# Two decoder layers on one core: score matmuls of an attention pair first, masks and decays after them, and a new table of priorities

## The chip, the cores and the metric

One Trainium2 chip, one of its cores. The metric is the device time of one execution in microseconds (us). The kernel before takes 358.33 us in the median of 3 runs (357.59 to 359.37).

## What is computed

Two layers over 256 tokens of width 1024. Each projects the modulated input to all queries, keys, values and gates, runs three kinds of attention head beside each other (DSA: 4 heads with an indexer that keeps the 64 best keys; FoX: 6 heads with a decay added to the scores; NSA: 6 heads with a compressed, a selected and a windowed branch), gates their output, projects it back and normalises.

```python
def hybrid_layer(x, c, ...):
    shift, scale, gate = jnp.split(c @ w_ada + b_ada, 3, axis=-1)
    u = x * (1.0 + scale[:, None, :]) + shift[:, None, :]
    h = split_cols(u @ w_in)
    ...
    o_dsa = dsa_mixer(dq, dk, h["dsa_v"], iq, ik, iw)
    o_fox = fox_mixer(fq, fk, fv, logf)
    o_nsa = nsa_mixer(grp(nq), grp(nq_rot), kc, vc, ks, kvs("nsa_vs"), kw, kvs("nsa_vw"), gates)
    mix = jnp.concatenate([o_dsa, o_fox, o_nsa], axis=-1)
    y = (mix * jax.nn.silu(h["gate"])) @ w_out
    return layer_norm(ALPHA * x + (1.0 + gate[:, None, :]) * y, ln_g, ln_b)
```

## The kernel before

**Weights.** All weights stream from HBM through SyncE's queue as tiles `raw` of up to 128x1024 (L497). ScalarE rounds each to `wh` (L528), VectorE takes the rest `wl = raw - wh` (L543), and every projection is three matmuls, h·H, l·H and h·L (L558, L559, L560). Some tiles are not matmul weights but rows of `w_ada`: VectorE multiplies them by `c` and sums them up (L592, called ada here).

**Stages.** In each layer come first the token-major projections (four chunks of columns), then 16 column-major weight tiles T0 to T15 (each 24 matmuls, shown in two halves of 12), between which the attention runs, and then the output projection: four blocks (two halves of the tokens by two halves of the width), each over four weight pieces that are called q0 to q3. Piece q reads the gated attention output `mH`, `mL` of head pairs 2q and 2q+1; for it VectorE multiplies the gate by the heads' output (L1165, L1173), ScalarE rounds to `mH` (L1176), VectorE takes `mL` (L1178).

**An attention pair.** `attn_pair` does two heads at once, 11 times in each layer: 6 pairs of NSA (three, each in two branches), 3 of FoX, 2 of DSA. Its scores are four matmuls over 64 rows (L756): for each half of the queries (t = 0 with 128 keys, t = 1 with 256) and each head a of the pair, in two PSUM tiles of 384 columns, one for each head. On them come, as matmuls over 96 or 128 rows in bf16, the decay (L761, FoX alone) and the mask (L766 for DSA, L768 for the others, 128 columns of the diagonal). In layer 1 the mask isn't a matmul: `vmask=('', 'dfn')` lets VectorE add it while it looks for the maximum (L697). Then follow exp on ScalarE (L703 or L714), the sum's reciprocal on VectorE (L685), the scaling (L727), the transposes (L737), their copy out of PSUM (L741) and the product with the values (L790). In an NSA pair the compressed branch is added last (L1128), and the output is copied to SBUF (L1010).

**What sets the order.** The whole program is recorded by a planner (`Order`): each step asks for an engine and states a duration, each task has a priority, and the planner always takes the step that can start first, by priority among those that can. The priorities, the limits of PSUM banks by use (`acc`, `s`, `side`), the order of the weight tiles (`tord0`, `tord1`), of the output's pieces (`oq0`, `oq1`) and the place of the ada tiles in the stream (`ada_at`) stand in the table `PR` (L373). What comes out is a fixed order on each engine; an instruction that waits holds up all behind it on its engine.

Of the kernel before, what the change touches and what calls it, by code (L numbers as in the profile page):

```python
# [18 lines left out]
P = 128  # L19
# [156 lines left out]
def bcast(ap, axis, n):  # L176
    return ap.unsqueeze(axis).to_broadcast([*ap.shape[:axis], n, *ap.shape[axis:]])
# [5 lines left out]
def stream_order():  # L183
    o = []

    def chunk(c, l):
        o.extend((c, l, q) for q in range(4))
# [10 lines left out]
    for l in range(DEPTH):  # L198
# [12 lines left out]
        else:  # L211
            for c in PR["cord"]:
                chunk(c, l)
        extra = []
        if l == 0:
            a, b = PR["ada_at"]
            extra += [(a + b * j, [("ada", 1, j, h) for h in range(2)]) for j in range(8)]
        a, b = PR["adag_at"][l]
        extra += [(a + b * j, [("ada", l, 2 * j + i, 2) for i in range(2)]) for j in range(4)]
# [18 lines left out]
class Order:  # L238
# [38 lines left out]
    def _unblock(self):  # L277
        moved = True
        while moved:
            moved = False  # L280
            for t in sorted(self.tasks, key=self._key):
# [6 lines left out]
                elif r[0] == "R":  # L288
# [3 lines left out]
                    if cls in ("s", "pt", "o", "ms", "ad"):  # L292
                        side = sum(self.used.get((tag, c), 0) for c in ("s", "pt", "o", "ms", "ad"))
                        if side + n > PR["side"]:
                            continue
# [19 lines left out]
    def run(self):  # L315
        while True:
            self._unblock()
            best = None
            for e in "PAVG":
                cand = [(t["ready"] + self.LAT[e], t) for t in self.tasks if t["req"][0] == e]  # L320
                if not cand:
                    continue
                first = max(self.free_at[e], min(r for r, _ in cand))
                r, t = min((z for z in cand if z[0] <= first + (PR["tol"] if self._key(z[1])[0] <= -2 else 0.02)),
                           key=lambda z: self._key(z[1]))
# [14 lines left out]
def pr(name, l):  # L340
    old = {"npair": ("nsa", 3), "dpair": ("dsa", 2), "fpair": ("fox", 3)}
    if name in old and name + str(l) not in PR:
        return [pr(old[name][0], l) + 0.01 * i for i in range(old[name][1])]
    return PR.get(f"{name}{l}", PR.get(name))
# [25 lines left out]

SCRATCH = 1024
RW = [11, 8]
PR = dict(irow=2, tout=(1, 1), tch=2, vmask=('', 'dfn'), zn='VA', upart=4, ul='VVVV', nrm='AAAA', cord='DCAB', t1q=0, cuts=(0, 512, 1024), oq=(0, 1, 2, 3), tord=(0, 1, 2, 3, 4, 5, 6, 7, 8, 9, 10, 11, 12, 13, 14, 15), gpp=(0, 1), res=-3.5, warm=10, tol=0.02, ada_at=(8, 0.5), adag_at=((0, 0.5), (8, 1)), ow=(512, 256), aff=3.14, tw=512, nact=((0, 0), (1, 0), (0, 1), (1, 1)), pro='', gp0=(0, 1), gp1=(0, 1), acc=4, s=3, pt=1, o=3, ms=3, side=7, topk=3, idx=2, dec=0.5, cmp=1.2, nsa=1.6, dsa=1.7, fox=1.8, gate=0.72, gate1=4.07, ada=9.04, main=10, ev=0, split=5, nahead=1, acc1=1.5, cmp1=2.15, dec0=0.36, nsa1=0.13, topk1=6.18, nsa0=1.72, dec1=1.66, idx1=0.56, tord1=(0, 4, 2, 7, 6, 1, 8, 9, 5, 3, 10, 12, 11, 13, 15, 14), dsa0=0.12, oq0=(3, 1, 0, 2), cmp0=1.01, fox1=1.95, dsa1=4.17, fox0=1.48, oq1=(1, 2, 3, 0), topk0=3.94, tord0=(0, 1, 3, 2, 4, 5, 6, 9, 7, 8, 10, 11, 12, 15, 14, 13), idx0=4.21, nrm1='AAAA', nrm0='AAAA', t1q0=0, t1q1=0, npair1=(-0.28, -0.61, -0.19), fpair1=(0.89, 8.92, 0.42), dpair0=(1.42, 0.27), dpair1=(4.85, 0.02), npair0=(3.8, 1.84, 4.78), fpair0=(1.21, 1.56, 1.31))  # L373


@with_exitstack
def trunk(ctx: ExitStack, tc: tile.TileContext, xT, x, crow, wst, bcol, lnrow, pe_b, cst, cstb, out,
# [3 lines left out]
    V, A, T, G = nc.vector, nc.scalar, nc.tensor, nc.gpsimd  # L381
# [14 lines left out]
    def nm(s):  # L396
        uid[0] += 1
        return f"{s}_{uid[0]}"

    def bank(cls, n=1):  # L400
        return ("R", "b", n, cls, CAP[cls])
# [7 lines left out]
    def until(*names):  # L409
        return ("U", names)  # L410

    def ps(*shape):
        n = int(np.prod(shape))
        t = pp.tile([P, 512], F32, tag="b", name=nm("b"), bufs=8)
        v = t[:, :n]
        if len(shape) == 2:
            v = v.rearrange("p (a b) -> p a b", b=shape[1])
        elif len(shape) == 3:
            v = v.rearrange("p (a b c) -> p a b c", b=shape[1], c=shape[2])
        return v  # L420
# [50 lines left out]
    ident_b = cb[:, 0:P]  # L471
    diag_b = cb[:, P:2 * P]
    esel_b = cb[0:96, 2 * P:2 * P + 6 * P].rearrange("p (h q) -> p h q", q=P)
# [272 lines left out]
    def attn_pair(l, kind, qT, kT, vs, obox, first, last, mask=None, cum=None, gate=None, prio=1):  # L746
        yield until(("raw", ("cb",)), ("raw", ("masks",)))
        yield bank("s", 2)
        onv = kind in PR["vmask"][l]
        yield ("P", 2 * fmm(128, 256) + (0 if onv else 0.35 if mask is not None else 0.24) + (0.35 if cum is not None else 0))  # L750
        sp = [ps(384) for _ in range(2)]
        for t in range(2):
            nk = P * (t + 1)
            for a in range(2):
                r = slice(64 * a, 64 * a + 64)
                T.matmul(sp[a][:, P * t:P * t + nk], qT[r, t * P:(t + 1) * P], kT[r, :nk], start=True,  # L756
                         stop=onv and cum is None, skip_group_check=True)
            for a in range(2):
                so = sp[a][:, P * t:P * t + nk]
                if cum is not None:  # L760
                    T.matmul(so, esel_b[:, cum[1] + a, :], cum[0][:, :nk], start=False, stop=onv,  # L761
                             skip_group_check=True)
                if onv:
                    continue
                if mask is not None:
                    T.matmul(so, ident_b, mask[:, P * t:P * t + nk], start=False, stop=True, skip_group_check=True)  # L766
                else:
                    T.matmul(so[:, nk - P:], ident_b, diag_b, start=False, stop=True, skip_group_check=True)  # L768
        vm = None if not onv else (causal[:, P:], causal) if mask is None else (mask[:, 0:P], mask[:, P:])
        nmx = small([P, 2, 2], "nmx", 6)  # L770
        st = small([P, 2, 2], "st", 6)
        evs = [(nm("exp"),) for _ in range(2)]
        ps_ = [[], []]
        for a in range(2):
            od.spawn(head_exp(sp[a], a, nmx, st, evs[a], ps_[a], vm), prio)
        yield until(*evs)
        yield ("V", 0.18 + (0.16 if gate is not None else 0))
        r = stats_finish(st, gate)
        evs = [(nm("head"),) for _ in range(2)]
        outs = [[], []]  # L780
        for a in range(2):
            od.spawn(head_pt(l, ps_[a][0], r, a, evs[a], outs[a]), prio)
        yield until(*evs)
        yield ("P", 0.85)
        if first:
            obox.append(ps(S))
        O = obox[0]
        for kt in range(2):
            for a in range(2):
                T.matmul(O[64 * a:64 * a + 64, P * kt:], vs(a, kt), outs[a][0][:, 256 * kt:256 + 128 * kt],  # L790
                         start=(first and kt == 0), stop=(last and kt == 1), skip_group_check=True)
        od.release("pT", 2)
# [6 lines left out]
    cum = small([96, S], "cum", 1, dt=BF16)  # L799
# [723 lines left out]
```

## Time and profile before

| | |
|---|---|
| median of 3 runs | 358.33 us |
| profiled execution | 361.92 us, span 360.1 us |
| TensorE busy | 338.1 us (94%), 2308 matmuls |
| VectorE busy | 306.7 us (85%), 757 instructions |
| ScalarE busy | 247.5 us (69%), 640 instructions |
| DMA | 76.51 MB, mean 212 GB/s |
| mean granted TensorE clock | 0.975 |

The profile is one execution. PE is TensorE, DVE VectorE, ACT ScalarE, SP SyncE. Matmuls overlap, so a matmul's listed duration is longer than the time to the next one's start; what one costs is read from the differences between starts. A group "x4" is several records that ran on from one another: a matmul in f32 over 64 rows leaves two records, one in bf16 leaves one. "Idle before" an instruction, with what ended it, is a wait; DVE, ACT and SP work through their rows in order, and so does PE.

### The profile page before, as it was taken

The page shows a single profiled execution, that of the slowest core. Times are in us where ns is not written, and L with a number is a line of the kernel's source. Part 1 is how long each engine was busy: PE and PEld are TensorE (multiplying, and loading weights), DVE is VectorE, ACT ScalarE, POOL GpSimd, SP SyncE. Part 2 cuts the span into 40 slices and gives each one's busy share as a digit, 9 for nine tenths or more (in the row PEclk, how much of TensorE's full clock was granted, in tenths as well). Part 3 has the DMA queues.
Part 4 walks back from the last instruction along what each step waited for, and adds up shares of the span by engine and source line. Part 5 has one row for each costly group of instructions (what it writes and reads, how often), then busy time and mean ns, then how long its engine had stood idle before and what let it go on. Part 6 is the DMA issues. An engine that isn't in the chain of part 4 may idle for free.

```text
span 360.1 us, 6567 instructions
## 1 busy us (share of the span) xinstructions
PE 338.1 (94%) x2308; PEld 275.4 (76%) x2308; DVE 306.7 (85%) x757; ACT 247.5 (69%) x640; POOL 2.5 (1%) x10
## 2 busy tenths in 40 slices
PE   5889999999999999997999999999999999999991
PEld 2668787888878776785888887868888997887890
DVE  4798997999997999999699898889899988467485
ACT  3446464996938888997086884657998857998120
POOL 2000000000000000000000000000000000000000
PEclk9899999999989999996999999999999999999997
DMA  7999999998736475550569386546587572403011
GB/s 218 408 407 406 407 380 392 410 412 331 233 96 212 164 237 174 177 167 0 155 183 308 114 300 206 177 124 192 161 283 238 181 230 60 116 2 117 3 58 58
DMA packets 22537, 76.51 MB, mean 212 GB/s; under 512 B 3028, under 2 KB 3432, under 8 KB 22376
## 3 DMA queue, kind: packets, MB, share of 16 engines
q1 hardware_dynamic: 22216, 75.80, 61.3%
q8 instruction: 18, 0.29, 0.3%
q10 hardware_dynamic: 288, 0.29, 0.2%
q14 instruction: 15, 0.12, 0.1%
HBM read 75.02 MB, written 1.06 MB: 211 GB/s over the span
## 4 chain that ended last, share of the span: by engine, by line
PE 36%; ACT 10%; DVE 5%; issue 1%; DVEq 0%; ACTq 0%
PE b L558 10%; PE b L560 10%; PE b L559 9%; ACT p L703 3%; ACT p L727 3%; DVE wl L543 2%; ACT wh L528 2%; PE b L790 1%; PE b L737 1%; PE b L941 1%; PE b L1045 1%; ACT pT L741 1%; PE b L670 1%; PE b L1418 1%; PE b L756 0%
## 5 line engine op out<-in xcount | busy, mean ns | idle before, releaser
L528 ACT CAST wh<-raw 128x1024 fp32r<-128x1024 f32 (+2 forms) x81 | 82.9, 1038 | 45.4 <-DMA raw<-in_wst_dram 22.1
L543 DVE TENSOR_TENSOR wl<-raw,wh 128x1024 fp32r<-128x1024 f32 (+2 forms) x81 | 96.4, 1195 | 14.2 <-ACT wh L528 12.4
L558 PE MATMUL b<-uH,wh 128*128 128x256 f32 x256 | 77.5, 303 | 0.8 <-ACT g L831 0.8
L560 PE MATMUL b<-uH,wl 128*128 128x256 f32 x256 | 72.6, 284 | 0.4 <-DVE wl L543 0.4
L559 PE MATMUL b<-uL,wh 128*128 128x256 f32 x256 | 72.4, 283 | 0.0
L592 DVE SCALAR_TENSOR_TENSOR raw<-raw,cbc 128x1024 f32<-128x1024 f32 x48 | 58.3, 1218 | 2.9 <-DMA raw<-in_wst_dram 2.5
L558 PE MATMUL b<-wh,uH 128*128 128x512 f32 (+1 forms) x128 | 51.1, 399 | 2.6 <-ACT uH L1398 2.6
L560 PE MATMUL b<-wh,uL 128*128 128x512 f32 (+1 forms) x128 | 50.4, 393 | 2.5 <-DVE uL L1400 2.4
L558 PEld LDWEIGHTS b<-uH,wh 128*128 128x128 f32 x256 | 48.9, 191 | 3.9 <-issue 1.5
L559 PE MATMUL b<-wl,uH 128*128 128x512 f32 (+1 forms) x128 | 49.9, 390 | 0.0
L560 PEld LDWEIGHTS b<-uH,wl 128*128 128x128 f32 x256 | 48.8, 191 | 0.7 <-DVE wl L543 0.7
L559 PEld LDWEIGHTS b<-uL,wh 128*128 128x128 f32 x256 | 49.0, 191 | 0.0
L727 ACT ACTIVATE p<-p,rinv 128x128 f32<-128x128 f32 (+1 forms) x88 | 34.1, 461 | 2.8 <-DVE rinv L685 1.4
L560 PEld LDWEIGHTS b<-wh,uL 128*128 128x128 f32 x128 | 24.4, 191 | 8.9 <-DVE uL L1400 4.6
L558 PE MATMUL b<-wh,mH 128*128 128x512 f32 (+1 forms) x80 | 29.3, 366 | 1.5 <-ACT mH L1176 1.5
L558 PEld LDWEIGHTS b<-wh,uH 128*128 128x128 f32 x128 | 24.4, 191 | 7.8 <-ACT uH L1398 3.2
L560 PE MATMUL b<-wh,mL 128*128 128x512 f32 (+1 forms) x80 | 29.2, 365 | 0.9 <-DVE mL L1178 0.9
L559 PE MATMUL b<-wl,mH 128*128 128x512 f32 (+1 forms) x80 | 28.7, 359 | 0.0
L559 PEld LDWEIGHTS b<-wl,uH 128*128 128x128 f32 x128 | 24.4, 190 | 4.3 <-DVE wl L543 0.3
L741 ACT COPY pT<-b 128x384 f32<-128x384 f32 x44 | 21.4, 489 | 4.7 <-PE b L737 4.5
L790 PE MATMUL b<-pT,vall 128*64 128x256 f32 (+1 forms) x176 | 22.5, 339 | 0.7 <-ACT pT L741 0.7
L737 PE MATMUL b<-cf,p 128*128 128x128 f32 x132 | 22.9, 283 | 0.2 <-ACT p L727 0.2
(179 smaller groups left out, 541.6 us busy)
## 6 DMA issues: line engine op xcount, KB each, us to landing
raw<-in_wst_dram SPq DMA_DIRECT2D x120, 512.0 KB, 5.1
raw<-in_wst_dram SPq DMA_DIRECT2D x7, 480.0 KB, 9.9
lnr<-in_lnrow_dram SPq DMA_DIRECT2D x4, 512.0 KB, 7.3
raw<-in_wst_dram SPq DMA_DIRECT2D x4, 448.0 KB, 3.6
x_sb<-in_x_dram SPq DMA_DIRECT2D x1, 1024.0 KB
row<-gate SPq DMA_DIRECT2D x2, 512.0 KB, 6.0
xT_sb<-in_xT_dram SPq DMA_DIRECT2D x3, 256.0 KB, 10.5
out_dram<-x_sb SPq DMA_DIRECT2D x3, 256.0 KB, 2.2
```

The costliest lines, as they stand in the source:

```text
L528: A.copy(h[:, :n], loaded[key])
L543: (G if on_pool else V).tensor_tensor(lo[:, :n], raw, h[:, :n].bitcast(F32), op=ALU.subtract)
L558: T.matmul(o, ah, bh, start=start, stop=False)
L559: T.matmul(o, ah, bl, start=False, stop=False)
L560: T.matmul(o, al, bh, start=False, stop=stop)
L592: V.scalar_tensor_tensor(w, w, 1.0, cbc, op0=ALU.mult, op1=ALU.mult, accum_out=mods[l][:, j, h:h + 1])
L670: T.transpose(pt[:, i, :], lhs, ident)
L703: A.activation(p_sb[:, blk], p_sb[:, blk], AF.Exp, bias=nmx[:, t, a:a + 1], scale=-1.0, accum_out=st[:, t, a:a + 1])
L727: A.mul(blk, blk, r[:, t, a:a + 1])
L737: T.transpose(pt[:, i, :], p_sb[:, P * i:P * i + P], ident)
L741: A.copy(pT, pt.rearrange("p a b -> p (a b)"))
L790: T.matmul(O[64 * a:64 * a + 64, P * kt:], vs(a, kt), outs[a][0][:, 256 * kt:256 + 128 * kt], start=(first and kt == 0), stop=(last and kt ...
```

## The change

`attn_pair` issues the same four score matmuls first (t = 0 and t = 1 for both heads), and only then, head by head, the decays and the mask. A mask is now one matmul for each head instead of two: for DSA all 384 columns at once, for the others one matmul that repeats the 128 columns of the diagonal and writes them to columns 0 to 127 and 256 to 383 of the head's PSUM tile. Only the first score matmul of a tile has `start` set.

```diff
+        spans = [slice(0, P), slice(P, 3 * P)]
         for t in range(2):
-            nk = P * (t + 1)
             for a in range(2):
                 r = slice(64 * a, 64 * a + 64)
-                T.matmul(sp[a][:, P * t:P * t + nk], qT[r, t * P:(t + 1) * P], kT[r, :nk], start=True,
+                T.matmul(sp[a][:, spans[t]], qT[r, t * P:(t + 1) * P], kT[r, :P * (t + 1)], start=t == 0,
                          stop=onv and cum is None, skip_group_check=True)
-            for a in range(2):
-                so = sp[a][:, P * t:P * t + nk]
+        for a in range(2):
+            for t in range(2):
+                so = sp[a][:, spans[t]]
                 if cum is not None:
-                    T.matmul(so, esel_b[:, cum[1] + a, :], cum[0][:, :nk], start=False, stop=onv,
+                    T.matmul(so, esel_b[:, cum[1] + a, :], cum[0][:, :P * (t + 1)], start=False, stop=onv,
                              skip_group_check=True)
-                if onv:
-                    continue
-                if mask is not None:
-                    T.matmul(so, ident_b, mask[:, P * t:P * t + nk], start=False, stop=True, skip_group_check=True)
-                else:
-                    T.matmul(so[:, nk - P:], ident_b, diag_b, start=False, stop=True, skip_group_check=True)
+            if onv:
+                continue
+            if mask is not None:
+                T.matmul(sp[a], ident_b, mask, start=False, stop=True, skip_group_check=True)
+                continue
+            T.matmul(sp[a].rearrange("p (b n) -> p b n", n=P)[:, ::2, :], ident_b, bcast(diag_b, 1, 2), start=False,
+                     stop=True, skip_group_check=True)
```

The table `PR` gets other numbers for 26 of its entries, among them `acc` 4 to 5, `s` 3 to 2, `side` 7 to 8, `ada_at` (8, 0.5) to (11, 0.25), `ada` 9.04 to 7.25, `oq0` (3, 1, 0, 2) to (3, 0, 1, 2), the two tile orders and the priorities of most pairs. The durations that the planner assumes for a pair are left as they were. VectorE and ScalarE keep all their instructions and shapes; TensorE loses 22 matmuls with their weight loads, all of them masks of layer 0; SyncE keeps its 145 stream entries. Below, what the two recorded orders say in three places; the numbers behind names are buffers.

TensorE, one branch of an NSA pair in layer 0, before (L756 scores, L768 mask with its weight load):

```order
L756 MATMUL b_1522<-q_32_143,q_36_147 128x128
L756 MATMUL b_1523<-q_32_143,q_36_147 128x128
L768 LDWEIGHTS cb
L768 MATMUL b_1522<-cb 128x128
L768 LDWEIGHTS cb
L768 MATMUL b_1523<-cb 128x128
L756 MATMUL b_1522<-q_32_143,q_36_147 128x256
L756 MATMUL b_1523<-q_32_143,q_36_147 128x256
L768 LDWEIGHTS cb
L768 MATMUL b_1522<-cb 128x128
L768 LDWEIGHTS cb
L768 MATMUL b_1523<-cb 128x128
```

The same branch now (the mask is line 769 of the changed file):

```order
L756 MATMUL b_1521<-q_32_143,q_36_147 128x128
L756 MATMUL b_1522<-q_32_143,q_36_147 128x128
L756 MATMUL b_1521<-q_32_143,q_36_147 128x256
L756 MATMUL b_1522<-q_32_143,q_36_147 128x256
L769 LDWEIGHTS cb
L769 MATMUL b_1521<-cb 128x2x128
L769 LDWEIGHTS cb
L769 MATMUL b_1522<-cb 128x2x128
```

The engine goes once, not three times, from matmuls over 64 rows to those over 128 rows or back, and issues two masks, not four.

VectorE, end of layer 0, before: from the third `mL` (of piece q3) to the fourth and last (of q2). `sg` is a gate, `osb` a pair's output, L543 the split of a weight tile.

```order
L1178 TENSOR_TENSOR mL_1760<-sg_2074,mH_1759 128x512
L1173 SCALAR_TENSOR_TENSOR sg_2107<-sg_2107,osb_2116 128x256
L543 TENSOR_TENSOR wl_2134<-raw_1989,wh_2113 128x1024
L1173 SCALAR_TENSOR_TENSOR sg_2107<-sg_2107,osb_1227 128x256
L543 TENSOR_TENSOR wl_2145<-raw_2004,wh_2122 128x1024
L1178 TENSOR_TENSOR mL_1760<-sg_2107,mH_1759 128x512
```

The same stretch now (two lines further down in the file):

```order
L1180 TENSOR_TENSOR mL_1769<-sg_2014,mH_1768 128x512
L543 TENSOR_TENSOR wl_2085<-raw_1912,wh_2058 128x1024
L1167 SCALAR_TENSOR_TENSOR sg_2079<-sg_2079,b_1729 128x512
L543 TENSOR_TENSOR wl_2098<-raw_1931,wh_2087 128x1024
L543 TENSOR_TENSOR wl_2110<-raw_1994,wh_2096 128x1024
L1175 SCALAR_TENSOR_TENSOR sg_2079<-sg_2079,osb_2112 128x256
L543 TENSOR_TENSOR wl_2123<-raw_1997,wh_2102 128x1024
L1175 SCALAR_TENSOR_TENSOR sg_2079<-sg_2079,osb_1234 128x256
L543 TENSOR_TENSOR wl_2128<-raw_2012,wh_2114 128x1024
L1180 TENSOR_TENSOR mL_1769<-sg_2079,mH_1768 128x512
```

The `mL` of q3 has moved up, past three splits and a gate. The last `mL` stands where it stood: as many instructions are ahead of it in both orders; among them were 39 splits and 38 ada rows, now 40 and 37.

TensorE, end of layer 0, before: the last pair's values, its compressed branch, then the output projection, whose first six matmuls are piece q3.

```order
L790 MATMUL b_1887<-pT_2050,vall_135 64x256
L790 MATMUL b_1887<-pT_2077,vall_135 64x256
L790 MATMUL b_1887<-pT_2050,vall_135 64x128
L790 MATMUL b_1887<-pT_2077,vall_135 64x128
L1128 MATMUL b_1887<-pcT_152,vc_151 64x256 x2
L558 MATMUL b_2096<-wh_2030,mH_1759 128x512
L559 MATMUL b_2096<-wl_2059,mH_1759 128x512
L560 MATMUL b_2096<-wh_2030,mL_1760 128x512
```

The same place now:

```order
L792 MATMUL b_1897<-pT_2070,vall_135 64x256
L792 MATMUL b_1897<-pT_2076,vall_135 64x256
L792 MATMUL b_1897<-pT_2070,vall_135 64x128
L792 MATMUL b_1897<-pT_2076,vall_135 64x128
L558 MATMUL b_2052<-wh_2001,mH_1768 128x512
L559 MATMUL b_2052<-wl_2053,mH_1768 128x512
L560 MATMUL b_2052<-wh_2001,mL_1769 128x512
L558 MATMUL b_2052<-wh_2001,mH_1768 128x512
L559 MATMUL b_2052<-wl_2053,mH_1768 128x512
L560 MATMUL b_2052<-wh_2001,mL_1769 128x512
L1130 MATMUL b_1897<-pcT_152,vc_151 64x256 x2
```

Piece q3 now stands ahead of the compressed branch of the last pair, and pieces q0, q1, q2 follow in this order (before: q3, q1, q0, q2).

## Rows read from the trace of the kernel before

**Rows 1.** Stretches: us, then PE, PEld, DVE, ACT, POOL busy (count), PEclk, DMA share, GB/s.
```profile
140.00:160.00 20.00, 20.00 (x157) 16.33 (x156) 19.97 (x42) 18.89 (x55) 0.00 (x0) 1.00 0.57 181
172.00:184.00 12.00, 12.00 (x55) 9.90 (x54) 8.99 (x23) 3.08 (x5) 0.00 (x0) 1.00 0.56 163
301.00:330.00 29.00, 28.77 (x230) 23.82 (x228) 18.81 (x65) 28.83 (x85) 0.00 (x0) 1.00 0.24 67
```

**Rows 2.** Timeline of PE (start us, duration us), layer 0: an NSA branch, first and next.
```profile
91.37 0.49 PE L756 MATMUL b<-q,q 64*128 64x128 f32 x4
...
92.77 0.50 PE L737 MATMUL b<-cf,p 128*128 128x128 f32 x3
```

**Rows 3.** Timeline of PE, layer 0: a FoX pair.
```profile
82.51 0.49 PE L756 MATMUL b<-f,f 64*128 64x128 f32 x4
...
83.91 0.28 PE L761 MATMUL b<-cum,cb 96*128 96x256 bf16 x1
84.03 0.22 PE L768 MATMUL b<-cb 128*128 128x128 bf16 x1
84.09 0.27 PE L761 MATMUL b<-cum,cb 96*128 96x256 bf16 x1
...
84.26 0.49 PE L670 MATMUL b<-cf,chunk 128*128 128x128 f32 x3
```

**Rows 4.** Timeline of PE: a DSA pair of layer 0, FoX and DSA of layer 1.
```profile
137.15 0.49 PE L756 MATMUL b<-q,q 64*128 64x128 f32 x4
...
138.58 0.36 PE L558 MATMUL b<-uH,wh 128*128 128x256 f32 x1
...
298.05 0.49 PE L756 MATMUL b<-f,f 64*128 64x128 f32 x4
...
299.47 0.37 PE L558 MATMUL b<-uH,wh 128*128 128x256 f32 x1
...
312.84 0.93 PE L756 MATMUL b<-q,q 64*128 64x128 f32 x8
313.70 0.87 PE L790 MATMUL b<-pT,vall 128*64 128x256 f32 x8
```

**Rows 5.** Timeline of PE, layer 0's output projection, with waits.
```profile
161.80 0.65 PE L1128 MATMUL b<-pcT,vc 15*64 15x256 f32 x4
163.99 0.50 PE L558 MATMUL b<-wh,mH 128*128 128x512 f32 x1 [1.54 <-ACT mH L1176]
...
165.61 0.80 PE L560 MATMUL b<-wh,mL 128*128 128x512 f32 x1 [0.89 <-DVE mL L1178]
...
171.33 0.47 PE L558 MATMUL b<-wh,mH 128*128 128x512 f32 x1
...
184.14 0.39 PE L560 MATMUL b<-wh,mL 128*128 128x512 f32 x1
```

**Rows 6.** Timeline of DVE, the same place.
```profile
164.87 0.69 DVE L1178 TENSOR_TENSOR mL<-sg,mH 128x512 fp32r<-128x512 f32 x1
165.47 0.42 DVE L1173 SCALAR_TENSOR_TENSOR sg<-sg,osb 128x256 f32<-128x256 f32 x1
165.81 1.22 DVE L543 TENSOR_TENSOR wl<-raw,wh 128x1024 fp32r<-128x1024 f32 x1
166.94 0.42 DVE L1173 SCALAR_TENSOR_TENSOR sg<-sg,osb 128x256 f32<-128x256 f32 x1
...
168.41 0.69 DVE L1178 TENSOR_TENSOR mL<-sg,mH 128x512 fp32r<-128x512 f32 x1
```

**Rows 7.** Stretches of 2 us, columns as in the first group.
```profile
100.00:102.00 2.00, 2.00 (x13) 0.93 (x12) 1.81 (x9) 0.56 (x2) 0.00 (x0) 0.50 0.03 8
166.00:168.00 2.00, 2.00 (x6) 1.52 (x6) 2.00 (x3) 1.37 (x2) 0.00 (x0) 0.50 0.00 0
```

**Rows 8.** Waits of DVE, 90 to 140 us: total, times, longest.
```profile
DVE sg L1165 <- ACT sg L1163: 1.3, 1, 1.3
DVE rinv L685 <- ACT p L714: 1.1, 1, 1.1
```

More of the change, by code (lines that the diff above doesn't have):

```diff
@@ L372 @@
 RW = [11, 8]
-PR = dict(irow=2, tout=(1, 1), tch=2, vmask=('', 'dfn'), zn='VA', upart=4, ul='VVVV', nrm='AAAA', cord='DCAB', t1q=0, cuts=(0, 512, 1024), oq=(0, 1, 2, 3), tord=(0, 1, 2, 3, 4, 5, 6, 7, 8, 9, 10, 11, 12, 13, 14, 15), gpp=(0, 1), res=-3.5, warm=10, tol=0.02, ada_at=(8, 0.5), adag_at=((0, 0.5), (8, 1)), ow=(512, 256), aff=3.14, tw=512, nact=((0, 0), (1, 0), (0, 1), (1, 1)), pro='', gp0=(0, 1), gp1=(0, 1), acc=4, s=3, pt=1, o=3, ms=3, side=7, topk=3, idx=2, dec=0.5, cmp=1.2, nsa=1.6, dsa=1.7, fox=1.8, gate=0.72, gate1=4.07, ada=9.04, main=10, ev=0, split=5, nahead=1, acc1=1.5, cmp1=2.15, dec0=0.36, nsa1=0.13, topk1=6.18, nsa0=1.72, dec1=1.66, idx1=0.56, tord1=(0, 4, 2, 7, 6, 1, 8, 9, 5, 3, 10, 12, 11, 13, 15, 14), dsa0=0.12, oq0=(3, 1, 0, 2), cmp0=1.01, fox1=1.95, dsa1=4.17, fox0=1.48, oq1=(1, 2, 3, 0), topk0=3.94, tord0=(0, 1, 3, 2, 4, 5, 6, 9, 7, 8, 10, 11, 12, 15, 14, 13), idx0=4.21, nrm1='AAAA', nrm0='AAAA', t1q0=0, t1q1=0, npair1=(-0.28, -0.61, -0.19), fpair1=(0.89, 8.92, 0.42), dpair0=(1.42, 0.27), dpair1=(4.85, 0.02), npair0=(3.8, 1.84, 4.78), fpair0=(1.21, 1.56, 1.31))
+PR = dict(irow=2, tout=(1, 1), tch=2, vmask=('', 'dfn'), zn='VA', upart=4, ul='VVVV', nrm='AAAA', cord='DCAB', t1q=0, cuts=(0, 512, 1024), oq=(0, 1, 2, 3), tord=(0, 1, 2, 3, 4, 5, 6, 7, 8, 9, 10, 11, 12, 13, 14, 15), gpp=(0, 1), res=-3.5, warm=10, tol=0.02, ada_at=(11, 0.25), adag_at=((0, 0.5), (8, 1)), ow=(512, 256), aff=2.1, tw=512, nact=((0, 0), (1, 0), (0, 1), (1, 1)), pro='', gp0=(0, 1), gp1=(0, 1), acc=5, s=2, pt=1, o=3, ms=3, side=8, topk=3, idx=2, dec=0.5, cmp=1.2, nsa=1.6, dsa=1.7, fox=1.8, gate=0.69, gate1=3.42, ada=7.25, main=10, ev=0, split=5, nahead=1, acc1=1.5, cmp1=0.65, dec0=-0.17, nsa1=0.13, topk1=7.44, nsa0=1.72, dec1=0.47, idx1=0.42, tord1=(0, 7, 4, 6, 2, 1, 8, 9, 5, 3, 10, 12, 11, 13, 14, 15), dsa0=0.12, oq0=(3, 0, 1, 2), cmp0=1.13, fox1=1.95, dsa1=4.17, fox0=1.48, oq1=(2, 1, 3, 0), topk0=3.11, tord0=(0, 1, 3, 2, 4, 6, 5, 9, 7, 8, 11, 10, 12, 14, 15, 13), idx0=4.01, nrm1='AAAA', nrm0='AAAA', t1q0=0, t1q1=0, npair1=(-0.4, -0.19, 2.86), fpair1=(-0.22, 5.77, 3.69), dpair0=(1.78, 2.73), dpair1=(1.61, 2.59), npair0=(3.02, 1.75, 4.78), fpair0=(1.72, 0.16, 1.0))
 @with_exitstack
```

## Prediction

> **What bounds the kernel now.** I read the stretches first, to see which engine is full where, then the timeline of TensorE inside an attention pair for prices, and then the two timelines at the end of layer 0, where the full engines wait for each other. From 140 to 160 us TensorE, VectorE and ScalarE are all nearly full, VectorE with 19.97 of 20 us [rows 1]. What ends this stage is VectorE: TensorE is through with the attention of layer 0 at about 162.4 (161.80 + 0.65) and then stands for 1.54 us for `mH` and 0.89 us for `mL` [rows 5], while VectorE runs on without a gap to the last `mL` at 169.10 (168.41 + 0.69) [rows 6]. After that idleness TensorE's clock is at half (0.50, so 1.2 GHz) [rows 7]: from the third output matmul at 165.61 to the sixteenth at 171.33, 13 steps take 5.72 us; later, 56 steps to the last at 184.14 take 12.81 us, 0.229 us each [rows 5]. From 172 to 184 TensorE alone is full and VectorE has room (8.99 of 12) [rows 1]. Layer 1 is TensorE's nearly throughout, until ScalarE fills up as well from 301 to 330 (28.83 of 29) [rows 1].
>
> **The pairs.** Each price is the time from a pair's first score to the next instruction.
>
> - An NSA branch takes 1.40 us (91.37 to 92.77) [rows 2]. Without masks the eight score records take 0.86 us (312.84 to 313.70) [rows 4], and that stretch also holds the one change back to 128 rows. A bf16 matmul of 256 columns takes 0.12 us (83.91 to 84.03), one of 128 columns 0.06 (84.03 to 84.09) [rows 3]. So a branch will take 0.86 + 2 x 0.12 = 1.10, which saves 0.30; six of them 1.80.
> - A FoX pair of layer 0 takes 1.75 us (82.51 to 84.26) [rows 3] and will take 0.86 + 2 x (0.06 + 0.12 + 0.12) = 1.46: three save 0.87.
> - A DSA pair of layer 0 takes 1.43 us [rows 4] and will take 0.86 + 2 x 0.18 = 1.22: two save 0.42.
> - A FoX pair of layer 1 takes 1.42 us (298.05 to 299.47) [rows 4] and will take 0.86 + 2 x 0.18 = 1.22: three save 0.60. The other eight of layer 1 have no bf16 matmul and keep their price.
>
> That is 3.1 us off TensorE in layer 0 and 0.6 us in layer 1. The mask that is written in two blocks is in no row; its bounds are 0.12 us (the price of as many columns in one block, which is taken, since each block is as wide as today's) and, for the dear end, twice that.
>
> **What of it reaches the end of layer 0.** Not the 3.1 us themselves: VectorE sets the last `mL`, and it keeps every instruction. The same number stands ahead of that `mL` as before, one split more and one ada row less, which I cost at nothing. VectorE gains only what it waits less. In 90 to 140 us two waits of 1.3 and 1.1 us are listed [rows 8]; the second lies behind the stretch at half clock around 101 us [rows 7], where TensorE was late, the first behind a gate's tanh, which the new order puts elsewhere. I take half of the 2.4, so 1.2 us; the bounds are 0 (the new order only moves them) and 2.4 (both go). The last `mL` then ends at 167.9.
>
> The larger term is what TensorE does before that. In the new VectorE order five splits, one gate and two products lie between the third `mL` and the last; by the steps of 0.34 (165.47 to 165.81) and 1.13 (165.81 to 166.94), and 0.60 for `mL` and for the gate, which is as long [rows 6], the two start 0.60 + 5 x 1.13 + 0.60 + 2 x 0.34 = 7.5 us apart, where today it is 3.5. So the third `mL`, which lets piece q3 begin, starts 4.0 us earlier relative to the last, and by 167.9 TensorE can have done q3, q0, q1 and two matmuls of q2: 20 instead of about 10 (by 169.10 today). From the 21st to the 72nd are 51 steps x 0.229 = 11.7 us, which gives 179.6 at full clock.
>
> But TensorE, with 3.1 us less to do, still waits ahead of q3 or ahead of q2, as today, and so I expect the low clock again. Today it costs 5.72 - 13 x 0.229 = 2.7 us; the stretch of half clock from 100 to 102 is shorter, and its 2 us cost 1.0. I take 2.2, near the first, since part of the low clock now falls ahead of the last `mL`, and keep 0 to 2.7. So the 72nd output matmul starts at 179.6 + 2.2 = 181.8 instead of 184.14: 2.3 us earlier. From there TensorE leads and layer 1 follows by as much.
>
> **Layer 1.** 0.6 us less on TensorE; but ScalarE is full from 301 to 330 [rows 1] and has the same rows to do, so I take half, 0.3 us, with 0 and 0.6 as bounds. The last DSA pair now has one half of a weight tile (12 matmuls) less between its scores and its last product; where ScalarE is late, that cover is gone, for at most 12 x 0.12 = 1.4 us, by the step of a 256-column matmul [rows 3].
>
> **What costs nothing.** Sixteen ada loads of layer 1 go one to three weight tiles later into SyncE's queue and so let T8, T10 and T11 pass. The DMA share is 0.57 from 140 to 160 [rows 1] and 0 in the wait at 166 [rows 7], so loads have room there; were a weight tile late, its split and TensorE behind it would be. The other limits of banks act only through the order.
>
> **Sum.** 2.3 + 0.3 = 2.6 us off the profiled execution (361.92 us, 3.59 above the median); taken off the median of 358.33 that is 355.7 us.
>
> **Rivals.**
>
> - *The clock stays high.* If TensorE reaches q3 only just before its `mL`, and its gaps are short, the 2.2 us don't arise: 355.7 - 2.2 = 353.5 us. For it: the work ahead of q2 is now 18 matmuls, not 3. Against: the gap ahead of q2 is still 167.9 less the end of q1; with q3 from about 160.3 on, 18 steps and 0.65 us for L1128 end at 165.1, and it is near 2.8 us, as long as today's two gaps together. The Trainium skill, page "TensorE: Matmul & The Clock Gate", section "What's actually happening", says that the throttled state is the default and activity releases it. By that rule a wait in a new place brings the low clock back, which is the forecast; the half clock after today's gaps agrees [rows 7].
> - *The mask's two blocks cost what the merging saves.* If a mask that writes two blocks takes 0.24 us, the 18 of them (six NSA branches and three FoX pairs, two each) take 2.2 us back and layer 0 saves 0.9 on TensorE; VectorE's waits then stay, and 355.7 + 1.2 = 356.9 us. Against: each block alone is today's mask. The Trainium skill, page "PSUM — Partial Sum Buffer", section "Specifications (TRN2)", says that a non-contiguous access pattern slows matmuls significantly; taken to the letter it speaks against this edit. No row here has such an output, so nothing bears it out yet.
> - *q3 blocks the last pair, and the kernel gets slower.* L1128 of the last pair now stands behind q3 on TensorE. If the third `mL` ends as late as today (165.56), then four more matmuls (0.92), L1128 (0.65), the copy (0.4), and on VectorE product, split, product, split and `mL` (0.34 + 1.13 + 0.34 + 1.13 + 0.69) make the last `mL` end at 171.2, or 172.7 with the first two terms at half clock; 11.7 and 2.2 us later it is 186.6, which is 2.5 us late, less 0.3 for layer 1: 360.5 us. It decides from a third `mL` that ends after about 163.4. For it: the chain is new, and its only slack is the 4.0 us that VectorE's new order gives. Against: that order is fixed, and VectorE has had no gap there.
> - *The order doesn't change what it says* is excluded: the recorded order shows 22 masks fewer and the scores together.
>
> **Chances.** About 0.5%, 1.8 us, is what a measurement of this kernel can tell from no change: faster is below 356.5, slower above 360.1. Forecast 0.42 (355.7, spread about 1.5 by the bounds of VectorE's waits and of the clock: 0.29 faster, 0.13 same); clock stays high 0.18 (0.17, 0.01); mask blocks 0.18 (0.05, 0.13); q3 blocks 0.22 (0.08 same, 0.14 slower). Together 0.51 faster, 0.35 same, 0.14 slower. The range goes from 352.6 (the high clock with most of VectorE's 1.2 us more) to 360.4 (about where q3's blocking lies), with some 0.18 outside; the forecast's own range is 354.2 to 357.2.
>
> **What would show it.** Right: an NSA branch of layer 0 at about 1.1 us and a FoX pair at 1.46; VectorE full from 140 to the last `mL`, which ends near 168; about 20 output matmuls ahead of it; a stretch at 0.50 clock around it. Wrong: a mask's step of 0.2 us or more; TensorE waiting for anything but `mH` and `mL` at the end of layer 0; the last `mL` after 170; new waits of TensorE on L741 after 301 us.

## The result, and the profile after

The changed kernel takes 356.76 us (median of 11 runs, 356.39 to 357.42); the kernel before took 358.59 us beside it (11 runs, 356.99 to 361.62). The ratio is 0.9948, with a 95% interval of 0.9923 to 0.9974. The profiled execution of the changed kernel took 356.42 us with a span of 354.6 us, where that of before took 361.92 us with 360.1. So the two traces differ by 5.5 us and the medians by 1.8. That gap is the key to the rest: the profile shown of before was one of its slower executions.

The stretches of the changed kernel that answer to [rows 1] and [rows 7] (us, then busy time and count of PE, PEld, DVE, ACT, POOL, then the granted clock, DMA share, GB/s):

```profile
140.00:160.00 20.00, 18.12 (x138) 14.31 (x138) 19.96 (x40) 18.41 (x47) 0.00 (x0) 1.00 0.45 162
301.00:330.00 29.00, 28.84 (x210) 23.62 (x209) 16.96 (x46) 26.60 (x73) 0.00 (x0) 1.00 0.22 73
100.00:102.00 2.00, 1.43 (x13) 0.75 (x12) 1.76 (x10) 0.94 (x3) 0.00 (x0) 1.00 0.03 12
166.00:168.00 2.00, 1.98 (x9) 1.64 (x10) 2.00 (x2) 0.18 (x1) 0.00 (x0) 1.00 0.00 0
```

VectorE still fills the end of layer 0 (19.96 of 20 us), and TensorE now has room there (18.12). The two stretches that ran at 0.50, which is 1.2 GHz, now run at 1.00, which is 2.4 GHz.

The pairs, in the timeline of TensorE (start us, duration us): FoX, NSA and DSA of layer 0, then FoX of layer 1, each with the instruction behind it. They answer to [rows 2 to 4].

```profile
81.74 0.93 PE L756 MATMUL b<-f,f 64*128 64x128 f32 x8
82.60 0.34 PE L762 MATMUL b<-cum,cb 96*128 96x128 bf16 x2
82.77 0.27 PE L769 MATMUL b<-cb 128*128 128x256 bf16 x1
82.89 0.33 PE L762 MATMUL b<-cum,cb 96*128 96x128 bf16 x2
...
83.26 0.71 PE L943 MATMUL b<-q,q 32*128 32x128 f32 x8
...
88.77 0.93 PE L756 MATMUL b<-q,q 64*128 64x128 f32 x8
...
89.77 0.36 PE L558 MATMUL b<-uH,wh 128*128 128x256 f32 x1
...
133.75 0.93 PE L756 MATMUL b<-q,q 64*128 64x128 f32 x8
...
134.81 0.42 PE L558 MATMUL b<-uH,wh 128*128 128x256 f32 x1
...
292.19 0.93 PE L756 MATMUL b<-f,f 64*128 64x128 f32 x8
...
293.31 0.36 PE L558 MATMUL b<-uH,wh 128*128 128x256 f32 x1
```

By differences of starts: FoX 1.52 us (1.46 said), NSA 1.00 (1.10 said), DSA 1.06 (1.22 said), FoX of layer 1 1.12 (1.22 said). Part of such a difference belongs to the instruction behind the pair: an NSA branch takes 1.00 us with a weight tile behind it and 1.18 with its product. Compared with the same instruction behind, before and now, the pairs take 1.83 and 1.52 us (FoX), 1.49 and 1.18 (NSA with its product), 1.43 and 1.06 (DSA), 1.42 and 1.12 (FoX of layer 1). So a pair or branch saves some 0.31 us, this DSA pair 0.37. The mask in two blocks takes 0.12 us (82.77 to 82.89), as many columns in one block would.

The end of layer 0 on TensorE answers to [rows 5]:

```profile
157.87 1.25 PE L792 MATMUL b<-pT,vall 128*64 128x256 f32 x8 [1.79 <-ACT pT L741]
159.05 0.50 PE L558 MATMUL b<-wh,mH 128*128 128x512 f32 x1
...
160.64 0.65 PE L1130 MATMUL b<-pcT,vc 15*64 15x256 f32 x4
...
164.94 0.50 PE L558 MATMUL b<-wh,mH 128*128 128x512 f32 x1 [0.72 <-ACT mH L1178]
165.27 0.40 PE L559 MATMUL b<-wl,mH 128*128 128x512 f32 x1
166.02 0.50 PE L560 MATMUL b<-wh,mL 128*128 128x512 f32 x1 [0.35 <-DVE mL L1180]
...
177.71 0.39 PE L560 MATMUL b<-wh,mL 128*128 128x512 f32 x1
```

and on VectorE to [rows 6]:

```profile
157.13 1.29 DVE L1180 TENSOR_TENSOR mL<-sg,mH 128x512 fp32r<-128x512 f32 x2
...
165.28 0.69 DVE L1180 TENSOR_TENSOR mL<-sg,mH 128x512 fp32r<-128x512 f32 x1
```

The last `mL` ends at 165.97 (169.10 before). Exactly 20 output matmuls start ahead of its end: the 21st, at 166.02, is the one that waits for it. The last 512-column output matmul starts at 177.71 (184.14 before).

### The profile page after: what moved, and what is told of

It is laid out like the page before. It is cut to its first block, busy times and chain, and to the rows that moved or that the text cites. A ratio compares the mean times of both kernels' runs of the same rounds, so it can differ in the third digit from the quotient of the medians.

```text
span 354.6 us, 6531 instructions
## 1 busy us (share of the span) xinstructions
PE 331.1 (93%) x2286; PEld 271.1 (76%) x2286; DVE 305.9 (86%) x757; ACT 247.0 (70%) x640; POOL 2.5 (1%) x10
## 3 DMA queue, kind: packets, MB, share of 16 engines
HBM read 75.02 MB, written 1.06 MB: 215 GB/s over the span
## 4 chain that ended last, share of the span: by engine, by line
PE 32%; ACT 10%; DVE 6%; issue 2%; DVEq 0%; ACTq 0%
PE b L558 8%; PE b L559 8%; PE b L560 8%; ACT p L703 3%; DVE wl L543 2%; ACT p L727 2%; ACT wh L528 2%; PE b L792 1%; PE b L737 1%; PE b L943 1%; ACT pT L741 1%; PE b L1047 1%; PE b L670 1%; PE b L756 1%; PE b L1420 1%
## 5 line engine op out<-in xcount | busy, mean ns | idle before, releaser
L543 DVE TENSOR_TENSOR wl<-raw,wh 128x1024 fp32r<-128x1024 f32 (+2 forms) x81 | 96.1, 1193 | 14.0 <-ACT wh L528 11.8
L558 PE MATMUL b<-wh,mH 128*128 128x512 f32 (+1 forms) x80 | 28.5, 356 | 0.7 <-ACT mH L1178 0.7
L560 PE MATMUL b<-wh,mL 128*128 128x512 f32 (+1 forms) x80 | 28.0, 350 | 0.4 <-DVE mL L1180 0.4
L559 PE MATMUL b<-wl,mH 128*128 128x512 f32 (+1 forms) x80 | 27.8, 348 | 0.0
L737 PE MATMUL b<-cf,p 128*128 128x128 f32 x132 | 23.7, 283 | 0.9 <-ACT p L727 0.5
L792 PE MATMUL b<-pT,vall 128*64 128x256 f32 (+1 forms) x176 | 21.6, 339 | 2.1 <-ACT pT L741 2.1
```

Of the source, the lines that this page charges most:

```text
L543: (G if on_pool else V).tensor_tensor(lo[:, :n], raw, h[:, :n].bitcast(F32), op=ALU.subtract)
L558: T.matmul(o, ah, bh, start=start, stop=False)
L559: T.matmul(o, ah, bl, start=False, stop=False)
L560: T.matmul(o, al, bh, start=False, stop=stop)
L737: T.transpose(pt[:, i, :], p_sb[:, P * i:P * i + P], ident)
```

## The experiments

My theory was that the table moves the `mL` at the end of layer 0 and that the edit's own saving is mostly lost to VectorE. The rivals were that the edit is the gain, and that the clock is. The first four kernels ran side by side.

**The kernel before once more.**

> The kernel before, unchanged, for a second profile and the clock of its runs. Theory A (the half clock at the end of layer 0 belongs to the order of the work): the second profile shows a stretch at granted clock 0.50 between 160 and 172 us again, and TensorE's first out-projection matmul again some 1.5 us late; ratio 1.000. Theory B (the profile shown was one of the slow ones, by chance): no stretch at 0.50 there, span near 356 to 357 us, and the runs with the lower mean clock are the longer ones.

358.11 us (12 runs, 356.89 to 361.36). Its profile is another execution of the same program, 357.58 us, without a drop in either place:

```profile
100.00:102.00 2.00, 2.00 (x21) 1.50 (x18) 1.80 (x10) 0.88 (x3) 0.00 (x0) 1.00 0.03 8
166.00:168.00 2.00, 2.00 (x11) 1.65 (x10) 2.00 (x3) 1.86 (x2) 0.00 (x0) 1.00 0.00 0
```

TensorE waits as long for `mH` and `mL` as in [rows 5] (1.5 and 0.9 us), yet the clock stays at 1.00. So the half clock falls in some executions and not in others, and theory B holds for the profile shown. The last `mL` of this second profile, and its 21st and 72nd output matmul:

```profile
166.97 0.68 DVE L1178 TENSOR_TENSOR mL<-sg,mH 128x512 fp32r<-128x512 f32 x1
```

```profile
168.39 0.39 PE L560 MATMUL b<-wh,mL 128*128 128x512 f32 x1
...
179.95 0.39 PE L560 MATMUL b<-wh,mL 128*128 128x512 f32 x1
```

Against the execution of [rows 5, 6], this one has its last `mL` 1.45 us earlier (its end is at 167.65) and its last 512-column output matmul 4.19 us earlier (179.95). The first figure is the delay that the drop near 100 us hands on: of the two waits of VectorE in [rows 8], the one of 1.1 us for `p` is missing here. The other 2.74 us are the drop at the end of layer 0. At full clock the 21st output matmul starts at 168.39 without a wait, 0.74 us after the last `mL`, and 17 have started by its end, not 10.

The unchanged kernel beside it, the same program, had 359.37 us. Where drops come and go, two medians of one program can thus lie 1.3 us apart.

The 99 runs of the unchanged kernel in three comparisons, by their mean clock, show it as well: 16 below 0.9765 have a median of 361.19 us, 56 from there to 0.9855 have 359.38, and the 27 at 0.9855 or above have 357.93. The bands are rough, because the mean also holds the start, where the clock of the first 20 us was between 0.83 and 1.00 in the profiles. All 11 runs of the changed kernel are at 0.986 or above.

**The edit alone**: the new pair code, the old table (against the changed kernel; entries left out are marked by dots).

```diff
-... acc=5, s=2, ... oq0=(3, 0, 1, 2), ...
+... acc=4, s=3, ... oq0=(3, 1, 0, 2), ...
```

> New attn_pair with the old table: the order on the four engines is that of before but for the masks. Theory A (VectorE sets the last mL of layer 0, so TensorE's saving is lost there): pairs of layer 0 at 1.10, 1.46 and 1.22 us, but the first waits for mH and mL grow by about as much as was saved; 0.3 to 1.5 us faster than before (ratio 0.996 to 0.999). Theory B (the edit itself is the gain): as fast as the changed kernel, ratio 0.995 or less, and the table adds nothing.

359.69 us, ratio 1.0010 (0.9989 to 1.0032): it gains nothing that shows, less than theory A's range. The pairs do save what was said, and the waits for `mH` and `mL` at the end of layer 0 have not grown (1.54 and 0.90 us), as theory A had them. What is lost is clock, in two places. One is near 98 us, where a run of thin matmuls (64 rows and 15 columns, then 64 columns, then the 30-column compressed scores) is followed by the scores of a pair. First the undisturbed execution of before, then the edit alone:

```profile
96.40 0.29 PE L1066 MATMUL b<-hid,w_sb 64*64 64x15 f32 x4
96.62 0.55 PE L1070 MATMUL b<-w_sb,hid 64*96 64x64 f32 x4
97.10 0.87 PE L790 MATMUL b<-pT,vall 128*64 128x256 f32 x8
98.19 1.52 PE L1085 MATMUL b<-kc,q 128*128 128x30 f32 x12 [0.22 <-ACT kc L1074]
99.65 0.49 PE L756 MATMUL b<-q,q 64*128 64x128 f32 x4
```

```profile
95.72 0.87 PE L792 MATMUL b<-pT,vall 128*64 128x256 f32 x8
97.43 1.94 PE L1087 MATMUL b<-kc,q 128*128 128x30 f32 x12 [0.84 <-ACT kc L1076]
99.31 1.23 PE L756 MATMUL b<-q,q 64*128 64x128 f32 x6
```

TensorE arrives 1.38 us earlier (95.72 against 97.10), but `kc` comes from ScalarE only 0.76 us earlier, so the wait grows from 0.22 to 0.84 us. Of the 1.38 us, 0.75 are a lead that this execution has at its first pair already (81.79 against 82.54). The other 0.6 us are what the two pairs ahead of this place save, and all of that goes into the wait. The clock is at half from there, and again at the end of layer 0, in this kernel's stretches:

```profile
100.00:102.00 2.00, 2.00 (x12) 1.29 (x11) 1.76 (x10) 0.40 (x2) 0.00 (x0) 0.50 0.03 8
168.00:170.00 2.00, 2.00 (x6) 1.62 (x5) 2.00 (x3) 1.53 (x2) 0.00 (x0) 0.50 0.00 0
```

Of its 12 runs 11 have a mean clock of 0.980 or less; of the 30 of the unchanged kernel beside it, 15 have. The drop at the end of layer 0 is the dearer of the two, as the filled kernels below show.

**The table alone**: the old pair code, the new table (the opposite diff).

> Old attn_pair with the new table: order of VectorE, ScalarE and the queues exactly that of the changed kernel. Theory A: about 20 out-projection matmuls stand ahead of the last mL again, so most of the gain is here: 0.5 to 2 us faster than before (0.994 to 0.999), 0.3 to 1.5 us slower than the changed kernel; pairs at the old prices of 1.40, 1.75 and 1.43 us. Theory B (the edit is the gain): ratio 1.000 to 1.004.

357.48 us, ratio 0.9947 (0.9925 to 0.9969), the ratio of the whole change; 9 of 12 runs at 0.987 or above, and the slowest, 358.87 us, has the lowest clock (0.978). So theory A holds, and the table keeps the low clock away in most runs without the edit. The edit adds to it: this kernel is 0.72 us slower than the changed one, and 0.60 slower than the next kernel, which ran beside it with the scores first. In the traces its last `mL` ends 0.80 us later (166.77 against 165.97), although its first pair starts 0.13 us earlier. What the table does near 98 us shows in the changed kernel, in the same view:

```profile
93.36 0.55 PE L1072 MATMUL b<-w_sb,hid 64*96 64x64 f32 x4
93.84 0.55 PE L737 MATMUL b<-cf,p 128*128 128x128 f32 x3
...
95.64 1.50 PE L1087 MATMUL b<-kc,q 128*128 128x30 f32 x12
```

Three transposes and twelve full matmuls now stand between the two thin groups, and the second waits for nothing.

**Scores first, masks not merged.**

(Arguments left out are marked by dots here and below.)

```diff
-            if mask is not None:
-                T.matmul(sp[a], ident_b, mask, ...)
-                continue
-            T.matmul(sp[a].rearrange("p (b n) -> p b n", n=P)[:, ::2, :], ident_b, bcast(diag_b, 1, 2), ...)
+            for t in range(2):
+                if mask is not None:
+                    T.matmul(sp[a][:, spans[t]], ident_b, mask[:, spans[t]], ...)
+                else:
+                    T.matmul(sp[a][:, 2 * P * t:2 * P * t + P], ident_b, diag_b, ...)
```

> The changed kernel with scores first, but each mask matmul split again into the two of before (22 matmuls more, the same columns, no output in two blocks). Theory A (what the edit saves is the changing between 64-row f32 and 128-row bf16 matmuls, and the columns are the same): an NSA branch stays within 0.1 us of the changed kernel's, and the time within 0.5 us of it. Theory B (a matmul has a fixed price that merging saves, and the two-block output is cheap): 22 times some 0.06 us, about 1.3 us more on TensorE, and 0.5 to 1.3 us slower than the changed kernel. Theory C (the two-block output costs double): faster than the changed kernel by up to 2 us.

356.88 us (7 runs), 0.12 from the changed kernel; a FoX pair takes 1.52 us, as merged, and an NSA branch 1.06:

```profile
88.94 0.93 PE L756 MATMUL b<-q,q 64*128 64x128 f32 x8
89.80 0.40 PE L770 MATMUL b<-cb 128*128 128x128 bf16 x4
90.00 0.36 PE L558 MATMUL b<-uH,wh 128*128 128x256 f32 x1
```

Theory A holds. The same branch with the old pair code, in the kernel with the table alone, has a weight tile behind it too:

```profile
88.66 0.49 PE L756 MATMUL b<-q,q 64*128 64x128 f32 x4
...
90.03 0.36 PE L558 MATMUL b<-uH,wh 128*128 128x256 f32 x1
```

That is 1.37 us. So having the scores together saves 0.31 (1.37 to 1.06), merging the masks some 0.06 more (1.00); where the product follows, merging saves 0.01 (1.19 to 1.18). The branch of [rows 2] can't be set against the 1.00, since its transposes follow it.

**Is it the clock?** Dummy matmuls into a bank that is overwritten next keep TensorE at work where it is thin, and move no other instruction. The two places, for layer 0 only, are ahead of the first compressed scores (three dummies, five with the new pair code) and ahead of the first block's first piece of the output projection (seven):

```diff
+            for _ in range(3 if l == 0 and t == 0 else 0):
+                T.matmul(sw.rearrange("p (b n) -> p b n", n=P), ident_b, bcast(diag_b, 1, 4), start=True, stop=True, ...)
             for j in range(3):
                 T.matmul(sc[:, j], nrT[j][:, t * P:(t + 1) * P], kc_sb, ...)
...
                     mH, mL = mix
+                    for _ in range(7 if l == 0 and n == 0 and t == 0 and q == oq[0] else 0):
+                        T.matmul(acc.rearrange("p (b n) -> p b n", n=P), ident_b, bcast(diag_b, 1, 4), start=True, stop=True, ...)
```

Before, both places filled:

> The kernel before with ten dummy matmuls of 512 columns on TensorE and nothing else moved: three ahead of the twelve 30-column matmuls of the compressed scores near 98 us, seven ahead of the first out-projection matmul of layer 0, where TensorE waits 1.5 us for mH. Theory A (the half clock follows TensorE's thin stretches, and it is what makes before slow): no stretch at 0.50 in either place, mean clock of nearly all runs 0.983 or more, median near that of the runs of before without a drop, 357.9 us (ratio 0.996 to 0.997). Theory B (the drops come from outside this core's work, by chance): clocks of 0.975 to 0.980 in about as many runs as before, ratio 1.000 to 1.002.

357.41 us (356.78 to 357.84), ratio 0.9956 (0.9927 to 0.9985); all 12 runs at 0.988 or above. Ten dummy matmuls make the kernel before 2.0 us faster than the unchanged one beside it (359.39 us), about as much as the whole change. They fit into the waits; `mH` is no longer waited for:

```profile
160.74 1.69 PE L1378 MATMUL b<-cb 128*128 128x512 bf16 x7
162.33 0.50 PE L558 MATMUL b<-wh,mH 128*128 128x512 f32 x1
162.66 0.40 PE L559 MATMUL b<-wl,mH 128*128 128x512 f32 x1
163.95 0.50 PE L560 MATMUL b<-wh,mL 128*128 128x512 f32 x1 [0.89 <-DVE mL L1182]
```

The edit alone, with the place near 98 us filled:

> New attn_pair with the old table and five dummy matmuls of 512 columns ahead of the 30-column matmuls near 98 us, where TensorE waits 0.84 us for kc. Theory A: the drop near 98 us goes, that at the end of layer 0 stays in most runs: mean clocks near 0.984 in place of 0.979, about 1 to 1.5 us faster than the edit alone (358.2 to 358.7 us). Theory B: clocks and time as with the edit alone, 359.4 to 360 us.

359.00 us, slower than theory A's range: 0.7 us gained, not 1 to 1.5. The profile shows the first place at 1.00 and the second at half clock, and only one of the 12 runs lies above 0.984. So the place near 98 us is the smaller part.

The edit alone, both filled:

> As the last, with seven dummy matmuls also ahead of the first out-projection matmul of layer 0. Theory A: no drop in either place, clocks of 0.985 or more, 356.8 to 358.0 us: the edit then gives the 0 to 1 us that the masks save, and the table's gain over the edit alone is mostly the clock. Theory B: time and clocks as with the edit alone. Theory C (the table's order is worth its time at full clock as well): clocks high, and still 1 us or more slower than the changed kernel, 357.8 us or above.

356.93 us (356.45 to 357.81), all runs at 0.987 or above, within 0.2 us of the changed kernel. Theory C falls. In layer 1 the FoX pairs are shorter here than before, too, but a wait for `pT` grows. First the undisturbed execution of before, then this kernel, from 255 to 352 us (total, times, longest):

```profile
PE b L790 <- ACT pT L741: 0.3, 1, 0.3
PE b L792 <- ACT pT L741: 1.0, 2, 0.7
```

The changed kernel, filled near 98 us, as a control:

> The changed kernel with three dummy matmuls of 512 columns ahead of the 30-column matmuls. There is no drop there to take away, so theory A: within 0.5 us of the changed kernel (356.4 to 357.3), the 0.7 us of dummies lost in VectorE's cover at the end of layer 0. Theory B (dummies help or cost by something else than the clock): a change of 0.7 us or more either way.

356.81 us: nothing, as theory A says. So in this kernel dummies bring nothing where there is no drop to prevent.

The edit alone, only the end of layer 0 filled:

> New attn_pair with the old table and seven dummy matmuls ahead of the first out-projection matmul of layer 0 alone, none near 98 us. Theory A (two drops, each with its own price): the drop near 98 us stays, mean clock 0.978 to 0.981; since its delay of TensorE passes on to the end of layer 0, 0.5 to 1.5 us slower than with both places filled (357.4 to 358.4 us), and 1.3 to 2.3 us faster than the edit alone. Theory B (the first drop brings the second about): clocks and time as with the edit alone, 359.4 to 360 us.

357.47 us: the time of theory A, but not its clocks, since only 2 of 12 runs lie at 0.981 or below; the profile has no drop near 98 us although TensorE waits 0.86 us for `kc` there, as with the edit alone. So the first drop comes in a part of the runs. The four kernels with the new pair code and the old table make a square: filling the end of layer 0 gives 2.22 us (359.69 to 357.47) and 2.07 (359.00 to 356.93), filling near 98 us gives 0.69 and 0.54. Only 359.00 and 356.93 ran side by side; the unchanged kernel had 359.37, 359.39 and 359.25 us in the three comparisons. So the two places add as far as can be seen, and the second drop doesn't need the first: with the place near 98 us filled, it still comes.

**Does the order at the end of layer 0 decide?**

```diff
-oq0=(3, 0, 1, 2)
+oq0=(3, 2, 0, 1)
```

> The changed kernel with pieces of layer 0's out projection taken in the order q3, q2, q0, q1: the piece that needs the last mL comes second, so 6 and two matmuls stand ahead of that mL in place of 18 and two. Theory A (how many matmuls stand ahead of the last mL decides, as forecast): 12 x 0.229 = 2.7 us later at the end of the out projection, of which 1 to 2.7 us arrive at the end at full clock; with a wait of some 3.5 us in one piece the half clock comes back in most runs and adds 1 to 2.7: 357.8 to 362 us. Theory B (TensorE isn't the bound after the last mL): 0.5 us at most.

361.21 us, 4.45 more than the changed kernel, and slower than before (1.0046, 1.0020 to 1.0071). Theory A holds, with 8 of 12 runs at 0.980 or below; how the 4.45 us divide between the later start and the low clock this run doesn't show. TensorE stands in one piece ahead of q2, and the clock is at half behind it; timeline and stretch:

```profile
161.12 0.65 PE L1130 MATMUL b<-pcT,vc 15*64 15x256 f32 x4
165.42 0.79 PE L558 MATMUL b<-wh,mH 128*128 128x512 f32 x1 [3.64 <-ACT mH L1178]
```

```profile
166.00:168.00 2.00, 2.00 (x6) 1.21 (x5) 2.00 (x3) 0.66 (x1) 0.00 (x0) 0.50 0.00 0
```

**Layer 1's part of the table set back.** The stretch from the first affine matmul of layer 1 (L631) to the last output matmul is the same to 0.06 us in every trace with one table: 70.11 to 70.17 us with the old one (the kernel before in both profiles and filled, and the edit alone, filled or not), 70.81 to 70.83 with the new one. So the new table costs layer 1 some 0.7 us.

```diff
-gate1=3.42, cmp1=0.65, topk1=7.44, dec1=0.47, idx1=0.42, tord1=(0, 7, 4, 6, 2, ...), oq1=(2, 1, 3, 0), npair1=..., fpair1=..., dpair1=...
+gate1=4.07, cmp1=2.15, topk1=6.18, dec1=1.66, idx1=0.56, tord1=(0, 4, 2, 7, 6, ...), oq1=(1, 2, 3, 0), npair1=..., fpair1=..., dpair1=...
```

> The changed kernel with the table's ten entries for layer 1 alone set back to those of before; those for layer 0 and the common ones stay new. The traces show 70.8 us from the first affine matmul of layer 1 to the last output matmul with the new table and 70.1 with the old one, whichever mask edit. Theory A (the new table costs layer 1 some 0.7 us by the order on ScalarE): layer 0 ends as in the changed kernel, layer 1 takes 70.1 us again, 356.0 to 356.5 us, faster than both kernels. Theory B (the common entries, or work of layer 1 that is hidden in layer 0, set that stretch): 356.7 us or more.

356.13 us (355.50 to 357.08, 12 runs), ratio 0.9928 (0.9899 to 0.9957). The changed kernel's two ends of the stretch, and this kernel's:

```profile
275.54 0.28 PE L631 MATMUL b<-cf,mod 128*8 128x128 f32 x1
...
346.35 0.28 PE L560 MATMUL b<-wh,mL 128*128 128x256 f32 x1
```

```profile
276.57 0.28 PE L631 MATMUL b<-cf,mod 128*8 128x128 f32 x1
...
346.68 0.28 PE L560 MATMUL b<-wh,mL 128*128 128x256 f32 x1
```

70.11 us against 70.81, so the entries for layer 1 cause the 0.7 us; that ScalarE's order does, as theory A has it, wasn't shown, and which instruction gives them wasn't isolated. This kernel has the lowest median of all, by 0.63 us, which fits the 0.7; but it didn't run side by side with the changed kernel, and the intervals of their ratios overlap, so only its gain over the kernel before is settled. The two spans, 355.0 and 354.6 us, don't show it: this execution is 1.1 us behind at its first pair already (82.84 against 81.74).

## Why the prediction was right, and where it was not

The time, 355.7 us forecast and 356.76 measured, was inside the range and on the side forecast. That it lies so near is in part luck: errors of opposite sign stand behind it.

- **The pairs** were nearly right, and the saving is the grouping of 64-row and 128-row matmuls, as the branch without masks suggested. With transposes behind it, as in [rows 2], an NSA branch takes 1.09 us in the kernel with the edit alone (1.10 said), a FoX pair with what stands behind it in [rows 3] 1.43 (1.46 said). The DSA pair was said 0.16 too long and FoX of layer 1 0.10, so TensorE saves some 3.5 us in layer 0 and 0.9 in layer 1, where 3.1 and 0.6 were said. *The mask's two blocks* falls as a rival: 0.12 us each. Here the measurement differs from the sentence of the Trainium skill, page "PSUM — Partial Sum Buffer", section "Specifications (TRN2)", that a non-contiguous access pattern slows matmuls significantly: this output, two blocks of 128 columns, costs nothing that shows.
- **The last `mL`** came earlier than all of the bounds: 3.13 us before that of [rows 6] (169.10 to 165.97), where I took 1.2 and at most 2.4. Of this, 1.45 us are the drop near 100 us, which the second profile of before lacks too, and of the other 1.68 us, 0.80 are a lead that this execution has ahead of its first pair (81.74 against 82.54). The remaining 0.9 us are near the 1.2 said.
- **Ahead of the last `mL`** I said 20 matmuls in place of about 10, and measured 20. But the 10 are a figure of the low clock. In both orders 20 stand ahead of that `mL`, and in the undisturbed execution 17 have started by its end. So seven of the ten matmuls that I counted as gained were the low clock's.
- **The low clock** is the step that failed. I wrote that "I expect the low clock again" and kept 2.2 us; by their times (356.39 to 357.42 us) and mean clocks (0.986 or more) it came in none of the 11 runs, and the last 512-column matmul started at 177.71 instead of 181.8: 1.9 us earlier with the last `mL`, and 2.2 by the clock. I argued that the gap ahead of q2 would be near 2.8 us. From the end of q1, about 164.2, to the last `mL` it was 1.75 us, because that `mL` came at 165.97 and not at 167.9, and two matmuls of q2 ran inside it; TensorE waited for 0.72 and 0.35 us. So *The clock stays high*, to which I gave 0.18, is what happened. Its short gaps ahead of q2 were there; that TensorE reaches q3 only just before its `mL` was not, since q3 began 0.6 us after that `mL`, behind the new wait for `pT`. With q2 second a wait of 3.64 us stands there, and the half clock is back. A wait alone doesn't decide it: the undisturbed execution of before has the same waits as [rows 5] and no drop.
- **The base** is the second failure. I took 2.6 us off the median, after working them out on an execution 3.6 us above it, which had both drops. These make up 4.2 us of the difference to the undisturbed execution, and by the bands above some 27 of 99 runs of before seem to have neither. On the traces the change gave 5.5 us; against the undisturbed execution of before it gave 1.2 (spans 355.8 and 354.6). The medians lie between. The forecast came out close because a gain smaller than that of the traces was taken off a base that has the drops in a part of its runs only.
- **Layer 1** was wrong in sign: 0.3 us gained was said, 0.7 is lost. The edit gives nothing there (70.11 us with it, 70.12 without): with the old table TensorE's wait for `pT` grows from 0.3 to 1.0 us and takes most of the 0.9 that the pairs save. So ScalarE took more there than the half that I left it. And the new table costs 0.7 us.
- **What costs nothing**: a wait for anything but `mH` and `mL` at the end of layer 0 was to be a sign of being wrong, and there is one: 1.79 us for `pT` ahead of the last pair's product. ScalarE has no gap from 150 us until then, and its copies to `pT` now stand behind four casts. The wait costs nothing by itself: VectorE, which ends this stage, has no gap there.
- ***q3 blocks the last pair*** needed a third `mL` that ends after about 163.4; it ended at 158.42.

So where did the 1.8 us come from? With the clock kept up by dummies, the edit is worth 0.48 us (357.41 to 356.93, side by side), and the table 0.12 more (356.93 to 356.81, the changed kernel filled near 98 us), which is less than these medians can tell from nothing. That the table gains about as much in layer 0 as it costs in layer 1 is suggested by the kernel with layer 1 set back (356.13). The remainder, some 1.2 us of the 1.8, is half clock that no longer occurs. The 1.2 us between the two undisturbed traces speak for a larger share of the order, but 0.8 of them are there at the first pair, and there the profiles of either table differ by as much among themselves (81.38 to 82.59 us with the old one, 81.61 to 82.84 with the new one). That the drops cost this time was shown by the dummies, which alone bring the old code to 357.41. Why the same program drops in one execution and not in the next stays open.

## What to carry to other kernels

Before a sum is made on a profile, compare its time and mean clock with all runs: if it stands 1% above the median, find what it has that the others lack, and price the change against an execution without it too. A saving on an engine that then waits may be lost twice, as with the edit alone here: in the wait, and in the clock behind it. Look at what the engine does next and put full work between thin groups and waits, by order if possible. A few dummy matmuls in the waits are a cheap test of how much of a difference is clock.

## What the runs showed of the hardware that was not expected

The granted clock differs between executions of one program: after waits of 1.5 and 0.9 us at the end of layer 0 it was 0.50 in one profile of the kernel before and 1.00 in another. A drop costs what it delays downstream: 1.45 us for the stretch near 100 us, handed on through VectorE to the last `mL`, and 2.74 us for that at 166. From the last output matmul of layer 0 to the first affine matmul of layer 1 all 13 traces take 90.05 to 90.14 us: whatever varied between executions varied before it.
